# Hybrid decoder step on one core: the input projection in two 512-wide prompt tiles, with the sample tokens of two weight blocks taken together

## The chip, the cores and the metric

One core of a Trainium2 chip runs the whole layer. The time is device microseconds of one execution, as the median of several runs. Everything is fp32 at the interfaces; inside, large products run in a rounded fp32 format (F32R in the code) with each operand split into a high and a low part, and three products high x high, low x high, high x low in place of one. Small products stay plain fp32.

## The reference

1024 prompt tokens and 32 sample tokens (8 sequences of 4) go through one layer. Cut to what matters:

```python
h = rmsnorm(x, norm_g)                      # x: 1024 (prompt) or 32 (sample) rows of 1024
proj = h @ w_in                             # 1024 x 3584
q, fp, i, za, glu, zb = split(proj, [512, 1024, 1536, 2048, 3072])
q = silu(q); f = lb + (1 - lb) * sigmoid(fp); k = 1 - f
o_a, s_new = hgrn2(q, k, i, log(f), s0)     # 4 heads of 128, a recurrence over tokens
o_a = rmsnorm(o_a) * silu(za)
glu = glu + b_glu
u = glu[:512] * sigmoid(glu[512:])
o_b = silu(layernorm(causal_dwconv(u))) * silu(zb)
y = rmsnorm(x + concat(o_a, o_b) @ w_out)
```

The same weights serve prompt and sample tokens.

## The kernel before

The normalised input is kept transposed, features on partitions, in four tiles `xT[hi/lo][half of the features]`, each with 1056 columns: 1024 prompt tokens and then 32 sample tokens. The columns of `w_in` that make the values `i` are multiplied token-major at the start (`v_block`, eight of them, into the banks `ops` and `ptps`). The other 24 blocks of 128 columns are projected feature-major, one after another, in the order of `ORD` and then `za` and `zb`. For each block, `load_w` loads the raw weights (`wraw`, two buffers), casts them on ScalarE to the high part (`wh`, two buffers) and subtracts on VectorE to the low part (`wl`, two buffers), one block ahead. `project` then runs three tiles of 352 tokens (3 x 352 = 1056, the last one holds the samples), with 8 feature slices x 3 products in each, 72 matmuls to a block, into three banks `mm` of four. At the end of the block the banks are evacuated by `evac` in the order 2, 0, 1: an activation on ScalarE (`act_into`, `glu_evac`), or on VectorE for the first half of the gated unit. The activation tables are switched around this batch.

Between the tiles `pump` emits pieces of other chains: the recurrence of a head (`hgrn`, a generator in `hq`), and the depthwise convolution and layer norm (`conv`, `ln_main`, in `bg`). How far the background runs ahead is set by two counters, `V` and `T`, which add up the assumed cost of what has been emitted for VectorE and TensorE. A list scheduler of the framework then orders each engine's instructions from dependencies, priorities and its own costs. All engines run their queue in order; all loads and stores go through SyncE's queue.

In `hgrn`, small products of 32 rows use column tiles: four products run in four groups of 32 output partitions (`tile_position`). The function `col_tiles` does the same for the 32 sample tokens: at the start for the values (`vps`, from the raw weights `wraw` and `wl` and the plain fp32 sample columns `xsT`), and in `sample_out` at the end. `bones` is a constant 128 x 128 matrix with a one where the two indices are equal modulo 32. One product with it adds four groups of 32 partitions and turns them.

After the projections follow the output projection (512-wide products in the same `mm` banks), the residual and the final norm (`finish`).

In the profile nearly all matmuls and VectorE instructions have one line, that of the counting helper (L72), so they are told apart by their tiles: `mm<-big,wh` and `mm<-big,wl` 128x352 are the projection, `ops<-` and `ptps<-` 128x512 the V blocks, `mm<-` 128x512 the output projection, `aux<-raw,qz` the sample tokens' state products in column tiles.

Of the kernel before, what the change touches and what calls it, by code (L numbers as in the profile page):

```python
# [9 lines left out]
F32 = mybir.dt.float32  # L10
# [8 lines left out]
P = 128  # L19
# [6 lines left out]
MB = 352  # L26
KO = 8
# [17 lines left out]
# columns of the packed per-partition vectors  # L45
# [9 lines left out]
# masks: causal, then s/t pairs of each level 64..1, then the diagonal  # L55
# [33 lines left out]
def _pe_ns(name, a, k):  # L89
    rhs = k.get("rhs")  # L90
    n = _free(a[0])
    if rhs is None:
        return 109
    return max(107, n / 2.4) if rhs.dtype == F32R else max(60, 4 * n / 2.4)


def emit(nc, tc, h, fast, flag_out=None):
    HW = 6 if fast else 5
    with ExitStack() as ctx:
# [8 lines left out]
        def big(dt=F32, w=TOK):  # L108
            return pool.tile([P, 4, w], dt, tag="big", name="big", bufs=6)
# [25 lines left out]
        xT = [[big(F32R) for _ in range(2)] for _ in range(2)]  # [hi/lo][ko half]  # L135
# [5 lines left out]
        xsT = sb([P, KO, ST], "ho", 2)  # L141
# [11 lines left out]
        def prep_x(tb, xr, n):  # L153
# [8 lines left out]
            for hf in range(2):  # L162
# [8 lines left out]
                src = tp[:, 0 : 4 * n].rearrange("p (k t) -> p k t", t=n)  # L171
                hi = xT[0][hf][:, :, tb * P : tb * P + n]
                S.copy(hi, src)  # L173
                if tb == 8:
                    S.copy(xsT[:, 4 * hf : 4 * hf + 4, :], src)
# [19 lines left out]
        def col_tiles(ps, n, first, last, lhsT, w):  # L195
            # the 32 sample tokens fill one of the four column groups for each quarter of w
# [74 lines left out]
        # queries of the sample tokens, one zero-padded group of columns for each sequence  # L271
# [34 lines left out]
        def load_w(blk):  # L306
# [7 lines left out]
            return hi, lo  # L314
# [28 lines left out]
        def pump():  # L343
            for _ in range(HU):
                step(hq)
            while bg and V.ns < T.ns + LEAD * 1000:
                step(bg)
# [35 lines left out]
        def act_into(dst, func, bias=0.0):  # L383
            def f(nb, ps):
                return [S.activation(dst[:, nb * MB : (nb + 1) * MB], ps, func, bias=bias)]  # L385

# [6 lines left out]
        def hgrn(hd, q, k, g):  # L393
# [4 lines left out]
            for hf in range(2):  # L398
# [44 lines left out]
                # decayed keys towards the chunk's end, token-major  # L443
# [155 lines left out]
            # the four groups of partitions hold the parts (hi, hi, lo, lo) of the keys and  # L599
            # (hi, lo, hi, lo) of the values, so one product carries all four pairs  # L600
# [101 lines left out]
        def conv(c, u):  # L702
# [61 lines left out]
        def glu_evac(u, func, bias):  # L764
            us = u[:, UW:UEND].rearrange("p (b t) -> p b t", t=PAD + NS)

            def f(nb, ps):
                n = min(MB, SEQ - nb * MB)
                parts = [(u[:, PAD + nb * MB : PAD + nb * MB + n], ps[:, 0:n])]
                if n < MB:  # L770
                    parts.append((us[:, :, PAD:], ps[:, n:MB].rearrange("p (b t) -> p b t", t=NS)))
# [90 lines left out]
        for i, (kind, c) in enumerate(order):  # L862
# [11 lines left out]
            w = ws.pop(0)  # L874
            nd = 1
            if kind == "gb":
# [7 lines left out]
                    w, glu_evac(u, AF.Sigmoid, cols[:, C_BGLU + 4 + c : C_BGLU + 5 + c]), nd  # L884
                )
            elif kind == "ga":
                u = cur["u"]
                project(w, glu_evac(u, None, cols[:, C_BGLU + c : C_BGLU + c + 1]), nd)
# [6 lines left out]
                if c == 3:  # L895
# [5 lines left out]
                    bg.append(ln_main())  # L901
            elif kind == "f":
                kt = sb([P, TOK], "qkg", 5)
                g = sb([P, TOK], "qkg", 5)
                project(w, act_into(kt, AF.Sigmoid), nd)
# [10 lines left out]
            elif kind == "q":  # L916
                q = sb([P, TOK], "qkg", 5)
                project(w, act_into(q, AF.Silu), nd)
                hq.append(hgrn(c, q, cur["kt"], cur["g"]))
            elif kind == "za":  # L920
                z = silu_tile()
                project(w, act_into(z, AF.Silu), nd)
# [3 lines left out]
            else:  # L926
                z = silu_tile()
                zb.append(z)
                if c == 2:
                    while not ln_state["done"]:  # L930
# [5 lines left out]
                        nd,  # L936
# [282 lines left out]
```

## Time and profile before

| | |
|---|---|
| median of 3 runs | 519.82 us (519.53 to 519.88) |
| span of the profiled execution | 517.7 us |
| TensorE busy | 502.1 us, 97% |
| VectorE busy | 384.0 us, 74% |
| ScalarE busy | 275.6 us, 53% |
| GpSimd busy | 2.9 us, 1% |
| projection matmuls | 1728, all 128x352 |
| matmul records in all | 3404 (a plain fp32 product leaves two, all others one) |

The page gives one execution of its own, of which only the span is known; what lies around it is the difference to the runs' median, 2.1 us. Start times are from the span's start. In rows of the timeline the busy time of matmuls overlaps, since each is pipelined with the next; the time that a matmul takes from its engine is the distance to the start of the next one.

### The profile page before, as it was taken

How to read it: one execution, taken by the hardware profiler on the slowest of the kernel's cores; microseconds unless marked ns; L12 is line 12 of the kernel's file. 1: busy time of each engine (PE TensorE's matmuls, PEld its weight loads, DVE VectorE, ACT ScalarE, POOL GpSimd, SP SyncE). 2: the span in 40 equal slices, each digit the busy share in tenths (PEclk: the TensorE clock that was granted, in tenths of full speed). 3: DMA queues.
4: the chain of work that ended last, by engine and by line, in shares of the span. 5: the costliest groups of instructions: out<-in, count | busy, mean ns of one | idle time of the engine just before them, and what ended most of it. 6: DMA issues, size and time to landing. Idle time of an engine off the chain costs nothing.

```text
span 517.7 us, 8480 instructions
## 1 busy us (share of the span) xinstructions
PE 502.1 (97%) x3404; PEld 453.2 (88%) x3404; DVE 384.0 (74%) x721; ACT 275.6 (53%) x517; POOL 2.9 (1%) x20
## 2 busy tenths in 40 slices
PE   5999999999999999999999999999999999999992
PEld 5789999889999999989999999999999967788881
DVE  4872299998988369998999989979566767545432
ACT  5873343213866475654737644754757868343321
POOL 1000000000000000000000000000000000000000
PEclk9899999999999999999999999999999999999997
DMA  8734122200211204111151001221125370211111
GB/s 303 241 136 100 42 52 50 43 0 1 51 42 43 55 22 114 41 42 47 42 122 47 22 37 47 88 76 42 47 56 185 128 304 33 87 46 42 63 58 47
DMA packets 21854, 39.37 MB, mean 76 GB/s; under 512 B 10512, under 2 KB 11792, under 8 KB 21808
## 3 DMA queue, kind: packets, MB, share of 16 engines
q1 hardware_dynamic: 21808, 38.77, 24.2%
q8 instruction: 28, 0.46, 0.4%
q14 instruction: 18, 0.15, 0.1%
HBM read 31.52 MB, written 7.24 MB: 75 GB/s over the span
## 4 chain that ended last, share of the span: by engine, by line
PE 94%; DMA 2%; ACT 2%; DVE 1%; SPq 1%; issue 0%; DVEq 0%
PE mm L72 73%; PE ops L72 8%; PE ptps L72 8%; PE aux L72 5%; DMA wl<-wi 2%; ACT hw L156 1%; DVE qkg L72 0%; SPq L216 0%; ACT big L173 0%; ACT big L224 0%; SPq L150 0%; ACT ss L157 0%; ACT big L1078 0%; ACT qkg L1089 0%; DVE cq L72 0%
## 5 line engine op out<-in xcount | busy, mean ns | idle before, releaser
L72 PE MATMUL mm<-big,wh 128*128 128x352 f32 (+1 forms) x1280 | 325.0, 332 | 0.0
L72 PEld LDWEIGHTS mm<-big,wh 128*128 128x128 f32 x1280 | 224.2, 188 | 7.1 <-issue 0.4
L72 PE MATMUL mm<-big,wl 128*128 128x352 f32 (+1 forms) x640 | 212.4, 332 | 0.0
L72 PEld LDWEIGHTS mm<-big,wl 128*128 128x128 f32 x640 | 120.5, 188 | 3.8 <-issue 0.4
L72 DVE SCALAR_TENSOR_TENSOR big<-u,wsum,big 128x511 f32<-128x511 f32 (+14 forms) x60 | 44.3, 739 | 0.3
L72 DVE TENSOR_TENSOR wl<-wraw,wh 128x1024 fp32r<-128x1024 f32 x24 | 29.3, 1222 | 20.6 <-ACT wh L312 20.5
L72 DVE SCALAR_TENSOR_TENSOR big<-u,cols,big 128x511 f32<-128x511 f32 (+14 forms) x60 | 44.1, 737 | 0.0
L72 DVE SCALAR_TENSOR_TENSOR cq<-u,cols,cq 128x511 f32<-128x511 f32 (+13 forms) x56 | 41.1, 734 | 0.0
L385 ACT ACTIVATE qkg<-mm 128x352 f32<-128x352 f32 x48 | 19.2, 465 | 31.7 <-PE mm L72 31.6
L312 ACT CAST wh<-wraw 128x1024 fp32r<-128x1024 f32 x24 | 25.2, 1050 | 19.0 <-PE mm L72 10.3
L72 DVE TENSOR_TENSOR qkg<-mm,big 128x512 f32<-128x512 f32 x16 | 10.9, 689 | 30.9 <-PE mm L72 30.9
L72 DVE TENSOR_TENSOR hw<-hw,qkg 128x512 f32<-128x512 f32 (+1 forms) x64 | 32.7, 550 | 0.0
L72 PE MATMUL ops<-big 128*128 128x512 f32 (+1 forms) x128 | 26.4, 399 | 1.7 <-ACT big L224 1.7
L325 ACT ACT_TABLE_LOAD x20 | 25.7, 1283 | 0.3
L72 PE MATMUL mm<-vt,wl 128*128 128x512 f32 x64 | 25.0, 391 | 0.0
L72 PE MATMUL mm<-vt,wh 128*128 128x512 f32 x64 | 25.0, 393 | 0.0
L1078 ACT ACTIVATE big<-qkg 128x512 f32<-128x512 f32 x16 | 10.0, 628 | 23.7 <-DVE qkg L72 23.7
L72 PEld LDWEIGHTS ptps<-hw 128*32 128x32 f32 (+1 forms) x448 | 13.7, 113 | 8.6 <-issue 3.4
L72 PE MATMUL ptps<-big 128*128 128x512 f32 x64 | 20.9, 395 | 0.4 <-ACT big L173 0.4
L72 PEld LDWEIGHTS ops<-big 128*128 128x128 f32 (+1 forms) x128 | 14.8, 155 | 5.9 <-ACT big L224 1.9
L72 PE MATMUL ptps<-hw 128*32 128x32 f32 (+1 forms) x448 | 19.7, 210 | 0.0
L385 ACT ACT_TABLE_LOAD x15 | 19.2, 1283 | 0.7 <-DVE hw L72 0.4
(226 smaller groups left out, 682.0 us busy)
## 6 DMA issues: line engine op xcount, KB each, us to landing
wraw<-win SPq DMA_DIRECT2D x24, 512.0 KB, 3.7
big<-xp SPq DMA_DIRECT2D x2, 2048.0 KB, 10.0
o_yp<-qkg SPq DMA_DIRECT2D x16, 256.0 KB, 2.3
wraw<-wo SPq DMA_DIRECT2D x6, 512.0 KB, 3.8
raw<-sh SPq DMA_DIRECT2D x4, 512.0 KB, 5.5
o_hs<-raw SPq DMA_DIRECT2D x4, 512.0 KB, 2.7
wh<-xp SPq DMA_DIRECT2D x3, 512.0 KB, 10.1
raw<-xp SPq DMA_DIRECT2D x2, 512.0 KB, 5.1
```

The source lines that it names most:

```text
L72: return f(*a, **k)
L156: S.activation(junk[0:n, :], xr[0:n, :], AF.Square, accum_out=sq[0:n, :])
L312: S.copy(hi, wr)
L325: after(S.preload_act_table_set("natural_log_exp_and_others"), prev)
L385: return [S.activation(dst[:, nb * MB : (nb + 1) * MB], ps, func, bias=bias)]
L1078: S.activation(xr[:, hs], y[:, hs], AF.Square, accum_out=sqs[:, half : half + 1])
```

## The change

The prompt part of the projection becomes two tiles of 512 tokens, 48 matmuls to a block, in two banks, and `xT` holds prompt tokens alone (its four tiles are in a pool of their own, `xt`). The sample tokens leave the split products. For each two blocks that follow each other, `samples` multiplies plain fp32: the 32 sample columns `xsT` are the stationary side, the raw weights of both blocks the moving side, in four column tiles of 32 partitions (even and odd feature slices of the first block, even and odd of the second), 16 products, into a bank of their own. ScalarE copies the 128 x 128 sums to `sps`, and `samples_turn` makes of them, by one fp32 product with the constant `bsel` (128 x 64), the feature-major 128 x 32 columns of both blocks in the same bank. `samples` stands ahead of the second tile of the first block of two, `samples_turn` after four of that tile's eight feature slices. Both blocks then evacuate 512, 512 and 32 columns in the order 1, 0, 2. The raw weights of both blocks stay in `wraw` until the sample products. `pump` is called after the first tile, in the middle of the second and at the block's end. The layer norm's pieces are held back until all four heads are done, and the assumed costs of matmuls grow by 13 and 10 ns.

```diff
+TB = 512
-    return max(107, n / 2.4) if rhs.dtype == F32R else max(60, 4 * n / 2.4)
+    return max(107, n / 2.4 + 13) if rhs.dtype == F32R else max(60, 4 * n / 2.4 + 10)
...
-        xT = [[big(F32R) for _ in range(2)] for _ in range(2)]  # [hi/lo][ko half]
+        xT = [
+            [big(F32R, SEQ, "xt") for _ in range(2)]
+            for _ in range(2)
+        ]
...
+                if tb == 8:
+                    S.copy(xsT[:, 4 * hf : 4 * hf + 4, :], src)
+                    continue
                 hi = xT[0][hf][:, :, tb * P : tb * P + n]
                 S.copy(hi, src)
-                if tb == 8:
-                    S.copy(xsT[:, 4 * hf : 4 * hf + 4, :], src)
...
+        bsel = sb([P, 2 * ST], "bsel")
+        nc.gpsimd.memset(bsel, 0.0)
+        for j in range(2):
+            hp = slice(j * 64, j * 64 + 64)
+            nc.gpsimd.tensor_copy(bsel[hp, j * ST : (j + 1) * ST], bones[hp, 0:ST])
...
-            return hi, lo
+            return hi, lo, wr
...
-            while q:
+            while q and not (q[0] is late.get("ln") and len(hdone) < H):
...
+        def samples(wa, wb):
+            t = smp["t"] = mmbank()
+            for k in range(0, KO, 2):
+                for g in range(4):
+                    T.matmul(
+                        t[g * ST : (g + 1) * ST, 0:P],
+                        lhsT=xsT[:, k + g % 2, :],
+                        rhs=(wa, wb)[g // 2][:, k + g % 2, :],
+                        start=(k == 0),
+                        stop=(k == KO - 2),
+                        tile_position=(0, g * ST),
+                    )
+            smp["s"] = sb([P, P], "sps")
+            S.copy(smp["s"], t[:, 0:P])
+
+        def samples_turn():
+            T.matmul(
+                smp["t"][:, P : P + 2 * ST], lhsT=smp["s"], rhs=bsel, start=True, stop=True
+            )
+
-        def project(w, evac, ndrain, nbs=(2, 0, 1), more=()):
+        def project(w, evac, ndrain, wn=None, more=()):
             pss = []
-            for nb in range(3):
+            for nb in range(2):
                 ps = mmbank()
+                if nb == 1 and wn is not None:
+                    samples(w[2], wn[2])
                 i = 0
                 for ko in range(KO):
                     for a, b in ((0, 0), (0, 1), (1, 0)):
                         T.matmul(
-                            ps[:, 0:MB],
+                            ps,
                             lhsT=w[b][:, ko, :],
-                            rhs=xT[a][ko // 4][:, ko % 4, nb * MB : (nb + 1) * MB],
+                            rhs=xT[a][ko // 4][:, ko % 4, nb * TB : (nb + 1) * TB],
                             start=(i == 0),
                             stop=(i == 23),
                         )
                         i += 1
+                    if nb == 1 and ko == 3:
+                        if wn is not None:
+                            samples_turn()
+                        if ndrain:
+                            pump()
                 pss.append(ps)
-                if nb < 2 and ndrain:
+                if nb == 0 and ndrain:
                     pump()
+            c0 = P if wn is not None else P + ST
+            pss.append(smp["t"][:, c0 : c0 + ST])
             with tc.high_priority(HP):
                 last = None
-                for nb in nbs:
-                    for ins in evac(nb, pss[nb][:, 0:MB]):
+                for nb in (1, 0, 2):
+                    for ins in evac(nb, pss[nb]):
...
+            wn = ws[0] if i % 2 == 0 else None
```

Three places show how instructions stand now. The first is TensorE at the second half of the last head's prompt tokens: its scores (`ptps<-hw`, column tiles of 32 and 64) and its state products (`aux<-vt,ho`); `aux<-ho,avg` is a head's norm, `aux<-ident,hw` a transpose. Before:

```order
L72 MATMUL mm<-big,wl 128x352
L72 MATMUL mm<-big,wh 128x352 x2
L72 MATMUL ptps<-hw 64x64
L72 MATMUL ptps<-hw 32x32
L72 MATMUL aux<-ho,avg 128x512
L72 MATMUL ptps<-hw 32x32 x5
L72 MATMUL ptps<-hw 64x64
L72 MATMUL ptps<-hw 32x32 x4
L72 MATMUL aux<-vt,ho 128x128 x4
L72 MATMUL ptps<-hw 32x32 x2
L72 MATMUL mm<-big,wl 128x352
```

and after, where `mm<-wraw,xsT` are the sample products and `mm<-bsel,sps` is the turn:

```order
L73 MATMUL mm<-xt,wh 128x512
L73 MATMUL mm<-wraw,xsT 32x128 x6
L73 MATMUL aux<-ho,avg 128x512
L73 MATMUL aux<-ident,hw 128x128 x4
L73 MATMUL ptps<-hw 64x64
L73 MATMUL aux<-ho,avg 128x512
L73 MATMUL ptps<-hw 32x32 x6
L73 MATMUL ptps<-hw 64x64
L73 MATMUL ptps<-hw 32x32 x6
L73 MATMUL mm<-wraw,xsT 32x128 x10
L73 MATMUL mm<-xt,wh 128x512
```

The sixteen sample products stand in two parts, with the head's products, some in column tiles and some on the full array, between them.

The second is ScalarE between a cast of weights and the evacuation of head 1's forget gate. Before:

```order
L312 CAST wh<-wraw 128x1024
L435 ACTIVATE hw<-hw 128x512
L435 ACTIVATE sm<-sm 128x32
L460 COPY ho<-aux 128x512
L448 ACTIVATE hw<-qkg 128x128 x4
L385 ACT_TABLE_LOAD
L385 ACTIVATE qkg<-mm 128x352 x3
L325 ACT_TABLE_LOAD
```

and after:

```order
L322 CAST wh<-wraw 128x1024
L485 ACTIVATE sm<-sm 128x32
L510 COPY ho<-aux 128x512
L498 ACTIVATE hw<-qkg 128x128 x4
L379 COPY sps<-mm 128x128
L434 ACT_TABLE_LOAD
L434 ACTIVATE qkg<-mm 128x512 x2
L434 ACTIVATE qkg<-mm 128x32
```

The copy that the turn needs stands behind a cast of weights and the head's decay, and ahead of the block's evacuation, which has the sample columns as a third piece.

The third is SyncE's queue at the first weight loads (`masks`, `smask`, `sc`, `sh` are constants and states). Before:

```order
L309 DMA wraw<-win 128x1024
L255 DMA raw<-masks 128x128
L258 DMA raw<-smask 128x32
L879 DMA u<-sc 128x8x30
L577 DMA raw<-sh 128x1024
L309 DMA wraw<-win 128x1024 x2
L889 DMA o_cp<-u 128x30
```

and after:

```order
L260 DMA raw<-masks 128x128
L263 DMA raw<-smask 128x32
L930 DMA u<-sc 128x8x30
L627 DMA raw<-sh 128x1024
L319 DMA wraw<-win 128x1024 x2
L941 DMA o_cs<-u 1024x1x30
L940 DMA o_cp<-u 128x30
```

The third block's weights are no longer loaded ahead of the constants, but together with the fourth's, behind the first states.

More of the change, by code (lines that the diff above doesn't have):

```diff
@@ L106, in sb, with big @@
             return pool.tile(shape, dt, tag=tag, name=tag, bufs=bufs)
-        def big(dt=F32, w=TOK):
-            return pool.tile([P, 4, w], dt, tag="big", name="big", bufs=6)
+        def big(dt=F32, w=TOK, tag="big"):
+            return pool.tile([P, 4, w], dt, tag=tag, name=tag, bufs={"big": 2, "xt": 4}[tag])
         def bank(tag, bufs):
@@ L346, in pump @@
             while bg and V.ns < T.ns + LEAD * 1000:
+                if bg[0] is late.get("ln") and len(hdone) < H:
+                    break
                 step(bg)
-        def project(w, evac, ndrain, nbs=(2, 0, 1), more=()):
+        smp = {}
+        def samples(wa, wb):
[17 more added lines that the diff above has]
+        def project(w, evac, ndrain, wn=None, more=()):
             pss = []
-            for nb in range(3):
+            for nb in range(2):
                 ps = mmbank()
+                if nb == 1 and wn is not None:
+                    samples(w[2], wn[2])
                 i = 0
@@ L384, in f @@
             def f(nb, ps):
-                return [S.activation(dst[:, nb * MB : (nb + 1) * MB], ps, func, bias=bias)]
+                return [
+                    S.activation(dst[:, nb * TB : min(TOK, (nb + 1) * TB)], ps, func, bias=bias)
+                ]
             return f
@@ L767, in f @@
             def f(nb, ps):
[L768 to L771, printed above, removed]
+                if nb < 2:
+                    parts = [(u[:, PAD + nb * TB : PAD + (nb + 1) * TB], ps)]
+                else:
+                    parts = [(us[:, :, PAD:], ps.rearrange("p (b t) -> p b t", t=NS))]
                 out = []
@@ L900, in emit @@
                     bg.insert(len(bg) - 1, lnp())
-                    bg.append(ln_main())
+                    late["ln"] = ln_main()
+                    bg.append(late["ln"])
             elif kind == "f":
@@ L983, in emit @@
                 if ko == 4:
-                    hi1 = big(F32R, D)
-                    lo1 = big(F32R, D)
+                    hi1 = big(F32R, D, "xt")
+                    lo1 = big(F32R, D, "xt")
                 hi = hi1[:, ko - 4, :]
@@ L1065, in finish @@
             if tb % 4 == 0:
-                xres["t"] = big(w=D)
+                xres["t"] = big(w=D, tag="xt")
                 nc.sync.dma_start(
@@ L1094, in emit @@
         mixes = [split_mix(0), split_mix(1)]
-        pss = [[mmbank(), mmbank()] for _ in range(2)]
+        pss = [[mmbank(), mmbank()], [mmbank(), mmbank()]]
         for kos in (range(4), range(4, KO)):
```

16 lines of the change are left out of this document (8 added, 8 removed).

## The prediction, made before the changed kernel ran

> **What bounds the kernel now.** I read the page's busy lines and slices first, then the waits of TensorE, then the chain that ended last, in order of time.
>
> ```profile
> PE 502.1 (97%) x3404; PEld 453.2 (88%) x3404; DVE 384.0 (74%) x721; ACT 275.6 (53%) x517; POOL 2.9 (1%) x20
> ...
> PE   5999999999999999999999999999999999999992
> ...
> PEclk9899999999999999999999999999999999999997
> ...
> PE 94%; DMA 2%; ACT 2%; DVE 1%; SPq 1%; issue 0%; DVEq 0%
> ```
>
> TensorE (PE) is busy in every slice but the first and the last, at full granted clock, and is 94% of the chain. VectorE (DVE) is at 74% on average, so I looked at its fullest stretch, and at what TensorE ever waited for.
>
> ```profile
> 200.00:300.00 100.00, 100.00 (x793) 94.05 (x792) 93.88 (x184) 59.63 (x113) 0.00 (x0) 1.00 0.24 63
> ```
>
> ```profile
> PE ops L72 <- ACT big L224: 1.7, 1, 1.7
> PE mm L72 <- DVE avg L132: 1.6, 1, 1.6
> PE mm L72 <- DVE raw L72: 1.2, 1, 1.2
> PE ops L72 <- DVE qkg L72: 0.8, 1, 0.8
> PE ptps L72 <- ACT big L173: 0.4, 1, 0.4
> PE mm L72 <- ACT ho L175: 0.2, 1, 0.2
> ```
>
> The first row has PE, its weight loads, DVE, ACT in that order: between 200 and 300 us DVE is busy 93.88 us and still PE idles for nothing. The other six rows are all of PE's waits, 5.9 us, on tiles of the input norm and the first V products, which the change leaves alone. So there is no stall in the projections that the change could remove: what it gains or loses is TensorE's own sequence of instructions, plus any wait that it brings in.
>
> **Price of the prompt products.** Every matmul is followed by the next with its drain hidden, so the price is start to start. I take it from the chain, which gives long runs of one shape (start, length, count), and the counts from the groups by shape.
>
> ```profile
> L72 PE MATMUL mm<-big,wh 128*128 128x352 f32 x1152 | 285.5, 326 | 0.0
> L72 PE MATMUL mm<-big,wl 128*128 128x352 f32 x576 | 187.5, 326 | 0.0
> ```
>
> ```profile
> 56.66 22.97 PE mm L72 x144
> 79.86 7.72 PE mm L72 x48
> 97.25 5.52 PE ptps L72 x24
> 396.66 12.08 PE mm L72 x75
> 449.91 58.25 PE mm L72 x256
> ```
>
> The first two groups are the 1728 projection matmuls (24 blocks x 3 tiles x 24). Runs 1, 2 and 4 are 352 wide: 22.97/144 = 159.5 ns, 7.72/48 = 160.8 ns, 12.08/75 = 161.1 ns; together 42.77 us for 267, 160.2 ns. Runs 3 and 5 are 512 wide: 5.52/24 = 230 ns in a V block, 58.25/256 = 227.5 ns in the output projection. Before: 1728 x 160.2 = 276.8 us. After: 24 x 2 x 24 = 1152 matmuls x 227.5 = 262.1 us; I take the output projection's value because its run is ten times longer. Saving 14.7 us. Ends: 159.5 with 230 gives 275.6 - 265.0 = 10.6 us; 161.1 with 227.5 gives 278.4 - 262.1 = 16.3 us. Between the two widths the slope is 67.3 ns for 160 columns, 0.421 ns a column, which leaves 12.1 ns fixed in each matmul: the saving is 576 matmuls fewer (7.0 us) and 576 x 32 = 18432 sample columns fewer (7.7 us). So the samples cost 7.7 us of streaming today, and the change must carry them for less than 14.7 us.
>
> A rule of the Trainium skill speaks against even this saving: "TensorE: Matmul & The Clock Gate", section on the back-to-back issue gap, gives N/2.4 + 2.5 ns, 149.2 and 215.8 ns here. By it the saving would be 257.8 - 248.6 = 9.2 us. The rows above hold 160.2 and 227.5 ns, so the rows decide.
>
> **Price of the samples.** Twelve times, 16 fp32 products of 32 sample rows by 128 raw weight columns, in four column tiles. The same shape is in the trace: the V rows of the samples at the start, and the heads' state products between two projection matmuls.
>
> ```profile
> 21.97 1.08 PE L72 MATMUL mm<-wraw,ho 128*32 128x128 f32 x32 [0.24 <-ACT ho L175]
> 22.98 0.55 PE L72 MATMUL mm<-ident,wh 128*128 128x128 f32 x3
> ```
>
> ```profile
> 254.88 0.32 PE L72 MATMUL mm<-big,wl 128*128 128x352 f32 x1
> 255.13 0.64 PE L72 MATMUL aux<-raw,qz 128*32 128x128 f32 x16
> 255.70 0.59 PE L72 MATMUL mm<-big,wh 128*128 128x352 f32 x2
> 256.13 0.32 PE L72 MATMUL mm<-big,wl 128*128 128x352 f32 x1
> ```
>
> An fp32 product leaves two records, so x32 is 16 matmuls and x16 is 8. Sixteen take 22.98 - 21.97 = 1.01 us, eight 0.57 us: 0.44 us for eight more. What an interruption costs in all is seen around the eight: from 254.88 to 256.13 is 1.25 us for them and three 352-wide matmuls (3 x 0.16 = 0.48), so 0.77 us. Sixteen alone between projection matmuls: 0.77 + 0.44 = 1.21 us, of which 0.87 us are the products and 0.34 us is going into column tiles and out. Twelve groups: 14.5 us.
>
> **Price of the turn.** Twelve times one fp32 product 128x128 by 64 columns. Its neighbours are one of 128 columns and one of 1 column:
>
> ```profile
> 277.78 0.32 PE L72 MATMUL mm<-big,wh 128*128 128x352 f32 x1
> 277.94 0.38 PE L72 MATMUL ops<-pt,vt 128*128 128x128 f32 x2
> 278.08 0.41 PE L72 MATMUL mm<-big,wh 128*128 128x352 f32 x1
> 278.33 0.32 PE L72 MATMUL mm<-big,wl 128*128 128x352 f32 x1
> ```
>
> ```profile
> 449.40 0.39 PE L72 MATMUL mm<-hw,wh 128*128 128x512 f32 x1
> 449.63 0.28 PE L72 MATMUL aux<-ss,bones 128*128 128x1 f32 x2
> 449.77 0.47 PE L72 MATMUL mm<-vt,wl 128*128 128x512 f32 x1
> 450.08 0.39 PE L72 MATMUL mm<-vt,wh 128*128 128x512 f32 x1
> ```
>
> 0.55 - 0.32 = 0.23 us for 128 columns, 0.68 - 0.455 = 0.23 us for one: 64 columns cost the same between them. Twelve: 2.7 us.
>
> **Places in the order.** The scheduler sets most groups alone, some beside head products in column tiles (there the 0.34 us is shared), and some apart, with full-array work between their parts (there it is paid twice). Counted over the fast program, changes of the array's tiling rise from 149 to 184, 35 more; twelve lone groups would make 24. But seven of the 35 are between two kinds of tiles. At half of 0.34 us each for the 28 that enter or leave the full array, and less for the seven, it is 4.8 to 5.9 us against 12 x 0.34 = 4.1 us. I leave it at 4.1 us, since products that follow other column tiles overlap them, and keep +1.8 us for the range.
>
> **Waits that are added.** The turn needs ScalarE's copy of the sums, and it stands 12 matmuls (2.7 us) or more behind them; queued behind a late turn is all of TensorE. Weight loads start later, since the raw weights of two blocks are held until the sample products in the middle of the first of them.
>
> ```profile
> L656 ACT COPY kts<-aux x4: 243/254/267, 193.6 to 381.8; 128x128 f32<-128x128 f32 x4
> ```
>
> ```profile
> L72 DVE TENSOR_TENSOR wl<-wraw,wh 128x1024 fp32r<-128x1024 f32 x24 | 29.3, 1222 | 20.6 <-ACT wh L312 20.5
> ...
> L385 ACT ACTIVATE qkg<-mm 128x352 f32<-128x352 f32 x48 | 19.2, 465 | 31.7 <-PE mm L72 31.6
> L312 ACT CAST wh<-wraw 128x1024 fp32r<-128x1024 f32 x24 | 25.2, 1050 | 19.0 <-PE mm L72 10.3
> ...
> L325 ACT ACT_TABLE_LOAD x20 | 25.7, 1283 | 0.3
> ...
> wraw<-win SPq DMA_DIRECT2D x24, 512.0 KB, 3.7
> ```
>
> The copy is 0.25 us (first row: the same shape), on an engine 60% busy at worst. A tile of weights lands 3.7 us after its issue, now about 6 us ahead of the block's end, and its cast waits for that end already (the 19.0 us of idle); then cast and subtraction, 2.3 us, lie beside a block of 48 x 0.2275 = 10.9 us. If that cover went, the next block would start up to 2.3 us late. On SP only the next weights, conv outputs and head states stand behind the held load, none due within a block. PSUM: after a block ScalarE needs a table load (1.28 us) and two evacuations of at most 1.45 x 0.465 = 0.68 us; the first bank it must free is due 24 matmuls later, 5.5 us. In the last block three evacuations now come after the last matmul instead of one; the output projection's first bank is free and takes 12 matmuls, 2.7 us, which covers the next bank. The gate on the layer norm, the new costs in the clock for emission and the removed casts of the sample columns move DVE and ACT work that nothing on PE waits for; their price is 0, with -0.5 to +1.5 us kept for the start and tail. I cost all added waits at 0, with up to 1.5 us at each turn as the upper bound: evacuating a block with both table loads (2 x 1.28 + 3 x 0.465 = 4.0 us) less 2.7 us of cover.
>
> **Sum.** -14.7 + 14.5 + 2.7 = +2.5 us on a span of 517.7 us: 520.2 us. The median of the runs, 519.82 us, lies 2.1 us above the span, and I keep that: 522.3 us, 0.5% slower. What a measurement can tell from no change is about 0.2%, 1.04 us. The ends of the terms give +0.9 us (saving 16.3) and +8.4 us (saving 10.6, switches +1.8).
>
> **Rivals.**
> - The turns wait. If a third of them (four) wait the 1.5 us, 6 us more: 528 us. For it: ScalarE's queue is in order and carries batches tied to table loads. Against it: today's products that wait for ScalarE copies never stall PE after the start.
> - Faster: the groups ride with the heads' column tiles. If none paid the 0.34 us, the samples would cost 12 x 0.87 + 2.7 = 13.1 us, less than 14.7: 518.2 us. It decides from the point where seven of twelve do (2.5/0.34). Against it is the order, which has more changes of tiling, not fewer.
> - A wash: a 512-wide matmul in the projections at 226 ns, or 352 wide at 161.1 throughout, takes 1.6 us off: 520.7 us or less. The sign turns at 225.3 ns (2.5 us over 1152), which no run of the rows shows.
> - The fixed part of a matmul is small, so the saving is 9.2 us: +8.0 us, 527.8 us. It is a mechanism of this kernel only if the 12.1 ns above belonged to something other than the matmul; the two widths deny that. This is the Trainium skill's issue gap, as above.
>
> **Chances.** Forecast 0.59; turns that wait 0.12; small fixed part 0.02; wash 0.14; faster 0.13. Slower by over 0.2% is the first three, 0.73; within it 0.14; faster 0.13. For eight in ten the range runs from 519.2 us, which leaves out most of the faster case, to 526.5 us, which takes in the dear end of the terms but not four waiting turns.
>
> **What the changed profile would show.** PE still at 97% or more; 1152 matmuls 128x512 at 227 to 230 ns start to start; 12 groups of 32 records from the raw weights at 1.0 us each, the next matmul 0.2 us late; 12 turns at 0.23 us; no wait of PE on the copy. I am wrong if the 512-wide run is under 225 ns, if a group of sixteen takes under 0.9 us in all, or if PE shows waits after 30 us.

## The result, and the profile after

The changed kernel takes 532.76 us (median; 532.1 to 533.07), the kernel before 519.67 us on the same chip: ratio 1.025, interval 1.0238 to 1.0263. It is 13.1 us slower. The forecast was 522.3 us, with a range to 526.5. Where a later run had one execution at more than twice the time of its others (1243 us in one, 1708 us in another), its time below is the median of the others.

The page of the changed kernel: busy times, slices of PE and of its clock, and the chain that ended last.

```profile
PE 510.7 (96%) x3236; PEld 406.4 (77%) x3236; DVE 383.5 (72%) x715; ACT 277.0 (52%) x523; POOL 3.4 (1%) x23
...
PE   5999999999999999999999799999999999999992
...
PEclk9899999999999999999999989999999999999997
...
PE 88%; ACT 5%; DMA 3%; DVE 2%; issue 0%; SPq 0%; DVEq 0%; ACTq 0%
```

PE's share of the chain fell from 94% to 88%, and there is a dip in the 23rd slice. PE's waits, without those of the first 23 us, which the kernel before has too:

```profile
PE mm L73 <- ACT qkg L434: 1.9, 1, 1.9
...
PE aux L73 <- ACT cq L882: 1.0, 1, 1.0
PE aux L73 <- ACT ho L739: 1.0, 1, 1.0
...
PE mm L73 <- DVE cq L73: 0.3, 1, 0.3
```

These four are 4.2 us, two of them at 301 to 305 us and two at the layer norm near 437 us; after the start the kernel before had none. None of them is the turn waiting for its copy.

First the prices that the prediction worked out. A run of prompt products in the chain (start, length, count), and, from PE's timeline, a group in one piece and a turn, each between prompt products (start, busy time, line, tile):

```profile
157.24 5.49 PE mm L73 x24
```

```profile
45.13 0.39 PE L73 MATMUL mm<-xt,wh 128*128 128x512 f32 x1
45.45 1.08 PE L73 MATMUL mm<-wraw,xsT 128*32 128x128 f32 x32
46.46 0.50 PE L73 MATMUL mm<-xt,wh 128*128 128x512 f32 x1
46.80 0.40 PE L73 MATMUL mm<-xt,wl 128*128 128x512 f32 x1
```

```profile
50.90 0.40 PE L73 MATMUL mm<-xt,wl 128*128 128x512 f32 x1
51.13 0.33 PE L73 MATMUL mm<-bsel,sps 128*128 128x64 f32 x2
51.27 0.71 PE L73 MATMUL mm<-xt,wh 128*128 128x512 f32 x2
```

A prompt product is 5.49/24 = 228.8 ns (forecast 227.5; over 1152 of them 1.4 us more). From 45.13 to 46.80 are a group and two prompt products: 1.67 - 0.46 = 1.21 us (forecast 1.21). A turn costs 51.27 - 50.90 - 0.23 = 0.14 us, and the two products behind it take 0.71 where undisturbed ones take 0.62: 0.23 us in all (forecast 0.23). The price list holds.

What is not on it is seen elsewhere in the timeline, where the scheduler mixed a group with a head's products:

```profile
269.05 0.43 PE L73 MATMUL mm<-wraw,xsT 128*32 128x128 f32 x8
269.40 0.49 PE L73 MATMUL aux<-hw,kts 128*128 128x512 f32 x1
269.83 0.41 PE L73 MATMUL mm<-wraw,xsT 128*32 128x128 f32 x2
270.17 0.40 PE L73 MATMUL ops<-pts,vs 32*128 32x32 f32 x2
...
271.15 0.86 PE L73 MATMUL mm<-wraw,xsT 128*32 128x128 f32 x22
```

One group stands in three pieces of 4, 1 and 11 products. The piece of one takes 270.17 - 269.83 = 0.34 us, and a product inside a whole group 1.01/16 = 0.06. The twelve groups lie in 22 pieces, where products that only other column tiles interrupt for under 0.3 us count as one.

And there is the place of the dip: rows of the timeline with the idle time before them, and then a table by stages (stretch, length, busy PE, PEld, DVE, ACT, POOL, and the granted clock):

```profile
302.33 0.50 PE L73 MATMUL aux<-ho,avg 128*128 128x512 f32 x1 [0.98 <-ACT ho L739]
304.73 1.79 PE L73 MATMUL mm<-wraw,xsT 128*32 128x128 f32 x32 [1.90 <-ACT qkg L434]
```

```profile
300.00:304.00 4.00, 1.85 (x31) 1.20 (x27) 4.00 (x9) 2.81 (x4) 0.00 (x0) 1.00 0.03 8
304.00:306.00 2.00, 1.27 (x28) 1.27 (x32) 2.00 (x5) 1.98 (x5) 0.00 (x0) 0.73 0.19 50
306.00:308.00 2.00, 2.00 (x22) 1.26 (x14) 1.99 (x7) 1.61 (x8) 0.00 (x0) 0.50 0.25 25
308.00:312.00 4.00, 4.00 (x37) 3.19 (x36) 3.91 (x7) 1.91 (x3) 0.00 (x0) 0.96 0.64 254
```

PE waits for head 2's norm and for an evacuation that stands behind it, and behind a table load of 1.28 us, in ScalarE's queue. VectorE is busy in 11.9 of these 12 us. After the wait the granted clock is halved for about 3 us, and the group takes 1.79 us in place of 1.08.

### The profile page after: what moved, and what is told of

Its sections match the earlier page's. It is cut to its first block, busy times and chain, and to the rows that moved or that the text cites. A ratio compares the mean times of both kernels' runs of the same rounds, so it can differ in the third digit from the quotient of the medians.

```text
span 530.6 us, 8157 instructions
## 1 busy us (share of the span) xinstructions
PE 510.7 (96%) x3236; PEld 406.4 (77%) x3236; DVE 383.5 (72%) x715; ACT 277.0 (52%) x523; POOL 3.4 (1%) x23
## 3 DMA queue, kind: packets, MB, share of 16 engines
q1 hardware_dynamic: 21808, 38.77, 21.6%
## 4 chain that ended last, share of the span: by engine, by line
PE 88%; ACT 5%; DMA 3%; DVE 2%; issue 0%; SPq 0%; DVEq 0%; ACTq 0%
PE mm L73 67%; PE ops L73 8%; PE ptps L73 7%; PE aux L73 5%; DMA wraw<-wi 1%; DMA wraw<-wo 1%; ACT big L899 1%; DVE u L73 1%; ACT xt L1040 1%; ACT qkg L434 1%; ACT u L877 0%; ACT L434 0%; ACT wh L1093 0%; DVE xt L73 0%; DVE qkg L73 0%
## 5 line engine op out<-in xcount | busy, mean ns | idle before, releaser
L73 PE MATMUL mm<-xt,wh 128*128 128x512 f32 x896 | 288.9, 396 | 0.0
L73 PEld LDWEIGHTS mm<-xt,wh 128*128 128x128 f32 x896 | 166.8, 188 | 35.9 <-issue 2.2
L73 PE MATMUL mm<-xt,wl 128*128 128x512 f32 x448 | 176.9, 395 | 0.0
L73 PEld LDWEIGHTS mm<-xt,wl 128*128 128x128 f32 x448 | 84.2, 188 | 16.9 <-issue 0.6
L73 DVE TENSOR_TENSOR qkg<-mm,xt 128x512 f32<-128x512 f32 x16 | 11.0, 689 | 31.2 <-PE mm L73 31.2
L434 ACT ACTIVATE qkg<-mm 128x512 f32<-128x512 f32 (+1 forms) x48 | 19.3, 465 | 24.6 <-PE mm L73 24.6
L73 PE MATMUL ops<-big,xt 128*128 128x512 f32 x64 | 23.3, 436 | 2.4 <-ACT xt L180 1.7
L1130 ACT ACTIVATE xt<-qkg 128x512 f32<-128x512 f32 x16 | 10.1, 631 | 26.0 <-DVE qkg L73 26.0
L73 PEld LDWEIGHTS ptps<-hw 128*32 128x32 f32 (+1 forms) x448 | 14.4, 114 | 9.6 <-issue 4.2
L73 PE MATMUL ptps<-big,xt 128*128 128x512 f32 x64 | 20.7, 392 | 0.0
L73 PE MATMUL mm<-wraw,xsT 128*32 128x128 f32 x416 | 18.3, 286 | 2.2 <-ACT qkg L434 1.9
```

Source lines behind the costliest of these rows:

```text
L73: return f(*a, **k)
L434: S.activation(dst[:, nb * TB : min(TOK, (nb + 1) * TB)], ps, func, bias=bias)
L1130: S.activation(xr[:, hs], y[:, hs], AF.Square, accum_out=sqs[:, half : half + 1])
```

## The experiments

In the diffs, minus is the changed kernel (or the kernel before, where it says so). Times are medians; the kernel before ran beside each at 519.6 to 519.9 us.

**Theory A (cuts and waits are two separate losses) against theory B (the 512-wide stream itself is dear).** The groups in one piece by a priority (`HP` is 3000), and scattered by a small one (30 in place of `HP`):

```diff
                 if nb == 1 and wn is not None:
-                    samples(w[2], wn[2])
+                    with tc.high_priority(HP):
+                        samples(w[2], wn[2])
```

> The sample products of a pair are given priority over what stands behind them, so that each group of sixteen stays in one piece (12 pieces, 23 in the changed kernel as it is); their arithmetic is the same. Theory A (a group in one piece costs its 1.2 us, a cut costs some 0.3 us more each time, and PE's waits at 301 to 305 us and at 435 us are a separate loss): 11 cuts x 0.3 = 3.3 us less, and another 3.3 us if the group no longer stands behind the waiting head products: 526 to 529.5 us. Theory B (cuts are free, what was lost is in the 512-wide stream itself): 532 to 533 us.

> The opposite of the run before: the sample products have a small priority, which scatters them among prompt products, 56 pieces where the changed kernel has 23. Theory A: 33 more cuts x 0.3 us = 10 us more, about 543 us. Theory B: no dearer than 534 us.

Measured: whole groups 536.88 us (ratio 1.0341, 1.0317 to 1.0365), slower than with the cuts; some 55 pieces 562.24 us (1.079 to 1.0836). Both theories missed both runs: whole groups came out 7 us above theory A's range, and the scattered ones lost three times what it said, if in its direction. The scattered ones show the price of a cut plainly:

```profile
39.80 0.49 PE L73 MATMUL mm<-xt,wl 128*128 128x512 f32 x1
40.22 0.41 PE L73 MATMUL mm<-wraw,xsT 128*32 128x128 f32 x2
40.56 0.49 PE L73 MATMUL mm<-xt,wh 128*128 128x512 f32 x1
40.98 0.41 PE L73 MATMUL mm<-wraw,xsT 128*32 128x128 f32 x2
```

From 39.80 to 40.56 are one prompt product and one sample product: 0.76 - 0.23 = 0.53 us for a product that costs 0.06 in company. The Trainium skill names a cause in "TensorEngine Tiling (Array Packing)", section Key Properties: changing the tiling mode drains the engine. The trace agrees in so far as each lone product costs 0.34 to 0.53 us; it shows the price and not the drain. So cuts do cost. But the run without cuts was slower still, and its PE waits were longer (two of them, below), so the waits are no separate loss of fixed size.

```profile
PE aux L73 <- ACT cq L883: 2.7, 1, 2.7
PE ptps L73 <- DVE hw L73: 2.2, 1, 2.2
```

**PE's load taken down.** The samples projected once, and groups with a quarter of their products:

```diff
+            if "kept" in smp:
+                return                  # in samples() and in samples_turn()
...
+            smp["kept"] = sb([P, 2 * ST], "kept")
+            S.copy(smp["kept"], smp["t"][:, P : P + 2 * ST])
...
-            pss.append(smp["t"][:, c0 : c0 + ST])
+            pss.append(smp["kept"][:, c0 : c0 + ST])
```

```diff
-            for k in range(0, KO, 2):
+            for k in range(0, 2, 2):    # with the priority of the whole groups
```

> The sample products and the turn are done for the first pair only; its 64 columns are copied to SBUF and evacuated for every later block, so the projections of the samples are left out for 22 blocks, and raw weights are no longer held there. Theory A: the 512-wide stream saves what the forecast said (13 to 15 us against before), and waits and cuts go with the groups: 519.8 - 14 + 1.5 = 507 us (505.5 to 509). Theory B (the 512-wide stream between heads' products is dearer than in its own long runs and saves half or less): 512 us or more. Theory C (the waits at 301 and 435 us come from the held weights or from the heads' own order, whatever the groups do) would leave up to 5 us of them: 510 to 512 us, with waits of PE in the trace.

> As the first run of these, but with the products of one pair of feature slices in four, four products in a group instead of sixteen; the sums lack the other slices. Going in and out of the column tiles, the turn, the copy and the held weights all stay. Theory A (54 to 63 ns a product in a group, the rest fixed): 12 x 12 = 144 products fewer, 7.8 to 9.1 us under the first run. Rival (the price of a group is mostly the change of tiling, the products overlap it): less than 4 us under it.

Measured: 537.51 us (1.0325 to 1.0362) and 540.28 us (1.0386 to 1.0441). Eleven groups and turns fewer, 16 us of PE's work, and the kernel is 4.8 us slower than the changed one; a quarter of the products, and 3.4 us slower than with all. All theories missed both. PE's waits in the run with the samples done once:

```profile
PE ops L73 <- DVE big L73: 6.2, 1, 6.2
PE aux L73 <- ACT cq L888: 6.1, 1, 6.1
PE ops L73 <- DVE st L73: 5.9, 2, 4.2
```

PE waits for heads (`st`), for the layer norm (`cq`) and for the gated output of both (`big`). So in this run the time is set by something other than the amount of PE's work.

**What is it? Theory D: VectorE's queue.** A third of the convolution left out, in three kernels; and a priority of 300 on the heads' steps, meant to put them ahead of it:

```diff
-            for i in range(14, -1, -1):     # the last of the convolution's three filters
+            for i in range(14, 14, -1):
```

```diff
             for _ in range(HU):
-                step(hq)
+                with tc.high_priority(300):
+                    step(hq)
```

> The run with the samples done once (537.5 us, 25 us of waits of PE on heads, layer norm and weights), and now also without the last 15 taps of the convolution of each channel group (60 VectorE operations, 44 us), which leaves wrong convolution outputs. Theory D (the heads' chain on VectorE, queued behind the convolution between 200 and 300 us, is as long as PE's own work; PE got ahead of it and then waits): the waits go, and the time is PE's own: 519.8 - 14 + 1.5 = 507 us, 505 to 511. Rival E (the waits come from banks, evacuations, tables or weights, not from VectorE's queue): above 525 us.

> The changed kernel with its sample products in whole groups (536.9 us), and without the same 15 taps of the convolution. Theory D: PE's own work alone, by the prices of the trace: 519.8 - 15.5 + 1.9 for the stream, + 12 x (1.21 + 0.24) for groups and turns = 523.6 us; 521 to 526. Rival E: 533 us or more.

> The kernel before, with the same 15 taps left out and with the line that holds the layer norm until the heads are done (which the shorter convolution needs). Theory D: PE never waited there, so nothing is gained: 518.5 to 521 us. Rival (VectorE bounds the kernel before too): 515 us or less.

> Nothing left out: the changed kernel with whole groups (536.9 us), and the heads' steps put ahead of the convolution and of the rest by a priority of 300. Theory D: the heads no longer queue behind the convolution, so PE's waits at 285 to 305 us go (5 to 8 us with the dip of the clock); the convolution ends later, and the layer norm may wait for it instead: 524 to 531 us. Rival E: 535 to 539 us.

Measured: 532.76 (1.024 to 1.0275), 533.28 (1.0251 to 1.0285), 522.44 (1.0045 to 1.0079) and 538.83 us (1.0355 to 1.039). Only 4.7 and 3.6 us come back, the kernel before gets 2.8 us slower, the priority brings nothing: by the numbers rival E is right in all three runs of the changed kernel, and theory D seemed to have fallen. But neither edit tested it. The priority did not do what it was meant to: by the trace, VectorE has done 77, 106 and 155 of the convolution's 176 tap operations before the scans of heads 0, 1 and 2, against 77, 106 and 151 without the priority. Why the lighter convolution did little shows in VectorE's share between the first norm and the end of head 1, in the run with the samples done once, then in the same with the lighter convolution:

```profile
169.80:281.90 112.10, 112.10 (x671) 90.21 (x672) 96.66 (x190) 59.95 (x110) 0.00 (x0) 1.00 0.18 55
```

```profile
162.80:280.00 117.20, 117.20 (x711) 93.55 (x710) 96.85 (x189) 61.42 (x112) 0.00 (x0) 1.00 0.17 54
```

VectorE does the same 97 us of work in both: with shorter convolutions, the next ones come earlier, and head 1 ends within 2 us of the same place. The dose was too small for the question.

A note on the kernel before: wherever convolution taps or sample parts are left out of it, it also has the changed kernel's line that holds the layer norm back until the heads are done.

**Theory F: the four heads, one after another, are a chain as long as PE's work.** Heads started 28 us earlier by another order of blocks; and three sample parts taken out of the chain:

```diff
-        ORD = "gb0 ga0 gb1 ga1 f0 q0 f1 q1 gb2 ga2 f2 q2 gb3 ga3 f3 q3"     # VPOS = 4
+        ORD = "gb0 ga0 f0 q0 gb1 ga1 f1 q1 gb2 ga2 f2 q2 gb3 ga3 f3 q3"     # VPOS = 2
```

```diff
             nc.sync.dma_start(s0, h["sh"][hd])
+            if hd > 0:
+                nc.sync.dma_start(h["o_hs"][hd], s0)
+                V.memset(late["mixa"][:, hd, SEQ:TOK], 0.0)
+                hdone.add(hd)
+                return
```

> The run with the samples done once (537.5 us), with the blocks in another order: forget gate and query of head 0 directly behind the first gated unit (gb0 ga0 f0 q0 gb1 ga1 f1 q1, the rest as it is; the V blocks move with f0). Nothing more is left out. Head 0 can then start some 30 us earlier. Theory F (the four heads run one after another, 20 to 24 us from norm to norm, and this chain with the layer norm and the output behind it is as long as PE's own work; with less work on PE it is the longer one): the chain ends up to 30 us earlier and PE bounds again, 507 to 513 us. Rival G (the waits come from PE's fixed order being wrong by some us at many places, whenever the chain starts): above 528 us.

> The changed kernel with whole groups (536.9 us) in the same other order, nothing left out. Theory F: PE's own sum by the prices of the trace, 523.6 us; 521 to 527. Rival G: above 532 us.

> The run with the samples done once, in its old order, and the sample part of heads 1 to 3 left out (their state is copied through, their sample columns are zero): 16 to 21 us of the chain each, but only about 3 us of PE's own time each. Theory F: the time falls by far more than PE's 9 us, to PE's own sum of 507 - 9 = 498 us (495 to 505), with few waits of PE. Rival G: about 537.5 - 9 = 528 us, at least 520.

> The kernel before with the same sample parts left out (and the line that holds the layer norm until the heads are done). Here PE has no waits after the start, so by both theories only PE's own time goes, 3 x 3 = 9 us: 508 to 513 us.

Measured: 536.62 (1.0304 to 1.0338), 538.46 (1.0337 to 1.0372), 499.58 (0.9592 to 0.9624) and 511.48 us (0.9824 to 0.9857). Shorter heads take 37.9 us off the one kernel and 8.4 us off the kernel before, as theory F said; PE does the same 87 matmul records less in both, 8.4 us of its busy time in the kernel before (502.1 to 493.7). So the chain is the bound of the first, and PE of the second. The other order did not help in either run, and missed theory F's range; VectorE's share, in the run with the samples done once, suggests why:

```profile
141.20:269.00 127.80, 127.80 (x760) 102.80 (x761) 120.70 (x232) 72.27 (x131) 0.12 (x1) 1.00 0.18 50
```

From the first norm to the end of head 1 it is busy 120.7 of 127.8 us. The heads start earlier and then share VectorE with more of the convolution.

**Was the kernel before at this bound already, and is it VectorE's queue (theory H)?** PE work that no head needs is taken out of the kernel before; and the taps of the prompt convolution out of four kernels:

```diff
-                    for a, b in ((0, 0), (0, 1), (1, 0)):
+                    for a, b in ((0, 0), (0, 1), (1, 0))[0 : 2 if cur['k'] in ('za', 'zb') else 3]:
```

```diff
-            for i in range(14, -1, -1):     # both loops of the convolution over its taps
-                ...
             S.activation(r, sm, AF.Identity, bias=cb2[:, c : c + 1], scale=tap(30))
-            ...                             # and the sums of the three filters
```

> The kernel before with PE work taken out that no head waits for: in the eight blocks za and zb the third product (low part of the input by high part of the weights) is left out, 8 x 3 x 8 = 192 matmuls of 160 ns, 30.7 us. Theory F (total = end of the last head's norm + 126 to 135 us in every run so far; before stands at 391.7 + 126): the heads' end hardly moves, PE waits instead, and the time falls by little: 508 to 520 us. Rival (PE's own work is the one bound before): 519.8 - 30.7 = 489 us, 487 to 495.

> The run with the samples done once (537.5 us), with all taps of the prompt convolution left out (some 175 VectorE operations, 130 us; the convolution outputs are wrong). Theory H (the heads are late because convolution operations stand ahead of theirs in VectorE's queue: 86 and 144 of 192 ahead of the first and second head in the changed kernel, 81 and 135 before): the chain of heads gets shorter and PE bounds, 505 to 511 us. Theory F alone (the chain of heads is long by its own steps, through ScalarE, PE's order and back): above 520 us.

> The changed kernel with whole groups (536.9 us), without the convolution's taps. Theory H: PE's own sum, 523.6 us, 521 to 526. Theory F alone: above 528 us.

> The kernel before, without the convolution's taps (and with the line that holds the layer norm until the heads are done). PE had no waits there: 517 to 522 us by either theory. It is the base for the two runs without convolution: their difference to it is the price of the change on PE alone, +2 to +4 us for whole groups, -11 to -14 us for the samples done once, if no waits are left in them.

> The kernel before with both left out: the third products of za and zb (30.7 us of PE, 523.0 us alone) and the convolution's taps (519.4 us alone). Theory H (PE and the heads behind the convolution in VectorE's queue are two bounds of the same length; each alone hides a saving on the other): with both shortened the time falls at last, to 519.4 - 30.7 = 489 us plus the waits for the layer norm that the other runs without convolution kept (2.6 and 6.7 us) and a dip of the clock: 490 to 502 us. Theory F alone: 515 us or more.

> The changed kernel as it is, its groups in pieces, without the convolution's taps. Against the same with whole groups (526.7 us) it has 12 more pieces (24 against 12), by theory A at some 0.3 us each: 526.7 + 3.6 = 530.3 us, 529 to 532. If cuts cost nothing: 526 to 528 us.

Measured:

| | with the convolution | without its taps |
|---|---|---|
| before | 519.7 | 519.38 (0.9989 to 1.0009) |
| before, 192 products fewer | 523.0 (1.0053 to 1.0086) | 491.78 (0.9433 to 0.9471) |
| samples done once | 537.51 | 515.4 (0.9905 to 0.9938) |
| changed, whole groups | 536.88 | 526.71 (1.0118 to 1.0152) |
| changed | 532.76 | 527.82 (1.0131 to 1.0165) |

The first two rows settle it. Taking 30.7 us of work from PE alone makes the kernel before 3.4 us slower (above theory F's 508 to 520 us, and far from the 489 us of PE as the one bound); taking 122.5 us from VectorE alone (384.0 to 261.5 us busy) changes nothing; both together give 27.9 us, inside theory H's 490 to 502 us. Two bounds of the same length lay side by side, and PE, the one without waits, hid the other. The line that holds the layer norm is in the right column of these rows and not in the left; that it makes no difference of this size is seen in the third row, where both kernels have it.

What PE waits for in the kernel before, once it has less to do (the three longest of 21.6 us after the start):

```profile
PE aux L72 <- ACT cq L832: 7.0, 1, 7.0
PE mm L72 <- ACT wh L1042: 4.3, 1, 4.3
PE ops L72 <- DVE big L72: 3.7, 1, 3.7
```

The waits are for the layer norm, a cast of the output's weights and the gated output, and 16.9 us of them lie behind the last norm of head 3. So the second bound is the heads with all that follows them. That the kernel is slower rather than equal goes with its lower mean granted clock, 0.95 against 0.99; how much that makes was not separated.

In the third row 22 us come back, but not all: PE still waits 6.7 us for the layer norm there, and without them it would be in its 505 to 511 us. The fourth row is 0.7 us above theory H's 521 to 526. The convolution's work on VectorE is thus the larger part of the delay, and the chain's own steps the rest. That it is the place in VectorE's queue that counts, and not the amount of work, is argued and was not separated. VectorE's work in the kernel before from the first norm to the end of head 1, and the same stretch without the taps:

```profile
165.30:265.80 100.50, 100.50 (x777) 93.14 (x776) 81.78 (x169) 58.58 (x110) 0.12 (x1) 1.00 0.19 53
```

```profile
163.60:252.70 89.10, 89.10 (x707) 81.98 (x706) 54.40 (x126) 53.44 (x108) 0.00 (x0) 1.00 0.18 51
```

Start of the mean product in the last norm of head 3, in the kernel before, the changed one, the one with the samples done once, and the kernel before with less work on PE:

```profile
391.65 0.18 PE L72 MATMUL aux<-ho,avg 128*128 128x32 f32 x1
```

```profile
402.24 0.28 PE L73 MATMUL aux<-ho,avg 128*128 128x32 f32 x1
```

```profile
407.39 0.18 PE L73 MATMUL aux<-ho,avg 128*128 128x32 f32 x1
```

```profile
387.72 0.40 PE L72 MATMUL aux<-ho,avg 128*128 128x32 f32 x1 [1.49 <-ACT ho L689]
```

To the ends of the spans (517.7, 530.6, 536.0, 521.0) it is 126.1, 128.4, 128.6 and 133.3 us: layer norm, gates and output projection. In the first three the time follows the end of the heads. It is no rule: in the fourth the heads end 3.9 us earlier than before and the span is 3.3 us longer, for the waits behind them, and with whole groups they end at 399.6 us, 2.6 us earlier than in the changed kernel, and the span is 3.8 us longer (534.4). In the same way (us):

| | before | changed | once | once, other order | before, less PE work |
|---|---|---|---|---|---|
| first norm of head 0 | 165.3 | 168.6 | 169.7 | 141.3 | 165.8 |
| last norm of head 0 | 200.2 | 208.4 | 208.0 | 189.3 | 200.7 |
| of head 1 | 265.8 | 279.1 | 281.8 | 269.2 | 266.3 |
| of head 2 | 335.6 | 346.3 | 350.3 | 350.3 | 334.4 |
| of head 3 | 391.7 | 402.2 | 407.4 | 408.1 | 387.7 |

The changed kernel loses its 10 us by the end of head 1, where VectorE is shared; the last head, with the convolution done, takes 56 us in the first two columns alike. In the order of VectorE's instructions more of the convolution stands ahead of the heads: of its 176 tap operations, at 0.74 us each, 72, 100 and 136 come before the scans of heads 0, 1 and 2 in the kernel before, and 77, 106 and 148 in the changed one. That these 5 to 12 operations alone make the delay was not tried with everything else equal. And up to 301 us PE has no wait on VectorE, so the delay is there in the order that the scheduler gave PE: before head 1's last norm stand 1035 of 1728 prompt products in the kernel before, 14.4 blocks, and 724 of 1152 in the changed one, 15.1 blocks. Together with the dearer samples this is the delay; why the scheduler set it so, the runs do not show.

What is left in the last two rows of the table is PE's own price. With whole groups PE still waits 2.6 us for the layer norm and 0.4 us elsewhere after the start, with the cuts 0.3 us:

```profile
PE aux L73 <- ACT cq L859: 2.6, 1, 2.6
...
PE aux L73 <- DVE cq L73: 0.4, 1, 0.4
```

```profile
PE aux L73 <- ACT cq L858: 0.3, 1, 0.3
```

So PE alone takes 526.7 - 3.0 = 523.7 us with whole groups, and 527.8 - 0.3 = 527.5 us with 23 pieces: 3.8 us for 11 cuts, 0.35 us each. This is an estimate. The medians themselves differ by 1.1 us, and the last run fell where "cuts cost nothing" had it (526 to 528 us), not in theory A's 529 to 532. The waits that are taken off are those of one execution, of 528.4 us, in which the granted clock also dropped behind them (0.50 in the row below); the others, at 526.5 to 526.7 us, are taken to have had the same waits.

```profile
432.00:434.00 2.00, 2.00 (x6) 1.52 (x6) 0.30 (x2) 1.95 (x4) 0.00 (x0) 0.50 0.01 4
```

The two kernels also differ in what stands around the groups, so the 3.8 us are what the cuts and their places cost together.

## Why the prediction was wrong

The direction came out, and the size did not: +13.1 us against +2.5.

- **The prices: right.** 228.8 ns for a prompt product, 1.21 us for a group, 0.23 us for a turn. Where little but these counts, with whole groups and no convolution, PE alone takes 523.7 us by the estimate above; the forecast was 522.3.
- **"I leave it at 4.1 us, since products that follow other column tiles overlap them": mis-sized.** The changes of tiling had been counted in the order, and the dear end kept at 1.8 us. By the same estimate the cuts cost 3.8 us more. A group that is split between full-array products pays each time (0.34 us for a single product).
- **"So there is no stall in the projections that the change could remove: what it gains or loses is TensorE's own sequence of instructions, plus any wait that it brings in": the step that failed.** It is true that PE did not wait, and the row that I quoted for it, VectorE busy 93.88 of 100 us "and still PE idles for nothing", was the warning, not the comfort. PE's queue was filled with blocks that no head needs, and they hid a second chain, through the heads, the layer norm and the output, that is as long as PE's work: 30.7 us less work on PE gave nothing. What the change did to the heads' end, 10.6 us later, I had priced at 0 ("DVE and ACT work that nothing on PE waits for"). It costs 5.0 us, the largest of the missing terms.
- **"I cost all added waits at 0": half right.** No turn waited for its copy, as said. The waits came in at head 2's norm, at an evacuation behind it and at the layer norm, which I had not looked at; the rival with waiting turns, 6 us, had nearly the size, by luck, since it had the wrong place. With the dip of the clock behind them they are 532.8 - 527.8 = 5.0 us, by the changed kernel with and without the convolution. My own sign of being wrong, waits of PE after 30 us, came true.
- **The range: too narrow by its own terms.** I wrote that 526.5 us "takes in the dear end of the terms"; that end is +8.4 us, which is 528.2 us, and the waits that I kept as an upper bound are not in it.
- **The sum:** 522.3, + 1.4 for the prices, + 3.8 for the cuts, + 5.0 for the heads, with 0.3 of waits that stay without the convolution, is 532.8 us. It closes because its terms are differences between the same runs; only the 1.4 us (1152 x 1.25 ns) has a second source. Read from the kernel before, PE's own work grew by 527.5 - 519.4 = 8.1 us, and the heads add 5.0.
- **The rivals.** The faster ones needed the groups to share changes of tiling; they are cut instead. The small saving by the issue gap did not come: a prompt product takes 228.8 ns, not 215.8.

No run points to a version faster than the kernel before: PE alone would need 523.7 us with whole groups, by the estimate, against 519.4.

## What to carry to other kernels

- An engine that never waits need not be the only bound. Before pricing a saving on it, follow the longest chain of work that passes through the other engines (here: heads, layer norm, output) and ask when it ends; work taken out of the busy engine in one trial run tells at once whether there is a second bound.
- When a change adds work to one engine's order, look at what the scheduler does with it: a batch that shares one change of mode is only cheap while it stays in one piece.
- An experiment that takes a load off must take off enough. A third of the convolution brought 4.7 us and seemed to clear VectorE; all of it brought 22.1. And a priority is only a test once the order that comes of it has been read.

## What the runs showed of the hardware

- The first full-array product after an interruption is followed 0.1 us late (46.46 to 46.80 is 0.34 us, where 0.23 is usual). Behind column tiles and behind a plain fp32 product it is alike: after the turn two products take 0.71 us in place of 0.62.
- Two short waits, 0.98 and 1.90 us with one product between them, were enough to halve the granted clock (0.50 from 306 to 308 us). The Trainium skill, "TensorE: Matmul & The Clock Gate", section What's actually happening, gives half the clock after an idle window of about 3.4 us; the half agrees, and here no single wait was that long. With whole groups and no taps, one wait of 2.6 us with one product behind it was enough (0.50 from 432 to 434 us, shown above).
